# Ordering background reduction sums behind weight splits on VectorE, and their pace in one stage, in a one-layer transformer kernel

## The chip, the cores and the metric

The kernel runs on 1 core of one Trainium2 chip, as one program. The metric is device time in microseconds (us) from start to end of an execution, median over runs.

## The reference, cut to what matters

One decoder layer with 256 positions of width 2048, all in float32. A conditioning vector `c` gives six modulation vectors, which scale and shift the input and gate the output of two sub-layers:

```python
mod = jax.nn.silu(c) @ w_ada[l] + b_ada[l]
sh1, sc1, g1, sh2, sc2, g2 = jnp.split(mod[:, None, :], 6, axis=-1)
h = x * (1.0 + sc1) + sh1
y = token_mixer(h, w_in[l], conv_w[l], a_log[l], dt_bias[l], gdn_norm_w[l], rel_bias,
                w_proj_moba[l], w_proj_gdn[l], w_out[l])
x = layer_norm(DEEPNORM_ALPHA * x + g1 * y, ln1_g[l], ln1_b[l])
h = x * (1.0 + sc2) + sh2
y = swiglu(h, w_ffn_in[l], w_ffn_out[l])
x = layer_norm(DEEPNORM_ALPHA * x + g2 * y, ln2_g[l], ln2_b[l])
```

`token_mixer` projects `h` with `w_in` (13344 columns) into the inputs of a softmax attention, a gated delta rule (GDN) and two gates, runs the two mixers, projects both, merges them with the gates and projects with `w_out`. `swiglu` has a width of 5632. The product `silu(c) @ w_ada` is a matrix (2048 x 12288, 100 MB) times one vector.

## The kernel before, in words

**Weights in two parts.** TensorE multiplies in a reduced float32 form, so every weight tile of 128 x 1024 elements (512 KB) is split. `load_w` (L212) loads it into one of five `raw` slots through the Sync queue (L215). `split_w` (L218) makes `hi`, a cast on ScalarE (L222), and `lo`, the low part, raw minus hi, on VectorE (L223); `hi` and `lo` have four slots each. A raw slot comes free when both have been made. The matmuls use hi and lo with a high and a low part of the activations: three matmuls where one would do.

**Steps.** The program is a list `prog` of steps (L279), one weight tile each: the first function loads and splits the tile, the second issues its matmuls (24 with 256 columns or 12 with 512) and calls `tick`. `run(3)` (L285) goes through the list and loads and splits tiles up to three steps ahead of the step whose matmuls are issued.

**Background work.** `tick` (L177) moves background generators on, one lane after the other: `moba` and `main` and `pre` (attention, GDN), then `ada`. After each piece of `ada`, that lane rests for `pace["gap"]` steps: gap 2 means a piece every second step. The gap is 2 at first, 1 from `merge_begin` (L1042), and 4 from `ffn_more` (L1282).

**The modulation sums.** `silu(c) @ w_ada` isn't done on TensorE. For each of 96 blocks of 128 columns, VectorE multiplies the transposed block with `cb`, which holds `silu(c)` on every partition, and sums along the row (`ada_sum`, L238, instruction at L242). The first 40 blocks come early, by `ada_opening` with whole blocks in buffers of their own. The other 56 come in halves of 128 x 1024 by the lane `ada`: `ada_sums` (L246) loads a half into a `raw` slot (L253), the same five slots that the weight tiles use, and issues the sum of the half loaded one piece before. That makes 112 sums. Five generators of eight blocks (80 sums) belong to the first sub-layer and the second modulation, one of sixteen blocks (32 sums) is queued in `ffn_more`.

**Who fixes the order.** The kernel's text gives a program order. A scheduler in the compiler then lays down, engine by engine, an order of instructions for good: it takes, by a model of durations, what it holds to be ready, the earlier in program order first. The chip executes each engine's instructions in that order. `keep_in_program_order` pins an instruction; a manual dependency without semaphore ("NoSync") between two instructions of one engine makes the scheduler place the one behind the other, and adds nothing to be executed.

**The stages**, in order of time: the opening (modulation of the first blocks and the first weight tiles of `w_in`), up to about 270 us; attention and GDN as background of the rest of `w_in` and of `w_proj_moba`; `w_proj_gdn` with the merge (from about 750 us; `merge_begin` after the eighth of its 32 steps); the output projection with `w_out` (from about 876 us), in blocks of 512, 512, 512, 256 and 256 columns; the feed-forward part. `out_begin` (L1079) stands ahead of the output projection: it finishes the first generator of `ada`, sends the gate `g1` as a row to DRAM and back to all partitions (L1074 to L1077, queue of GpSimd), and sets up buffers. `mod2` (L1113), ahead of the fourth block, drains the lane `ada` and works out the second modulation (L1115 to L1118).

Other lines that the text names: L585 and L589 (the decay of the GDN), L653 (squared norms of the GDN's q and k; it frees a PSUM buffer), L762 (matmuls of the GDN's triangular inverse), L868 (normalization of the GDN's output, 16 instructions in a row), L354 to L356 (matmuls with 512 columns), L305 to L307 (with 256).

Of the kernel before, what the change touches and what calls it, by code (L numbers as in the profile page):

```python
# [13 lines left out]
OP = mybir.AluOpType  # L14
# [78 lines left out]
def layer(ctx, tc, a, out):  # L93
    nc = tc.nc
    v_, s_, g_, t_, dma = nc.vector, nc.scalar, nc.gpsimd, nc.tensor, nc.sync
# [21 lines left out]
    cols = perm.tile([P, V_END], F32, name="cols")  # L117
# [9 lines left out]
    cb = perm.tile([P, D], F32, name="cb")  # L127
# [30 lines left out]
    adac = perm.tile([P, 96], F32, name="adac")  # L158
# [4 lines left out]
    pace = {"all": 1.8, "gap": 2, "debt": 0.0}  # L163
    done = set()

    def advance(lane):
        while bg[lane]:
            try:
                return next(bg[lane][0])
            except StopIteration:  # L170
                bg[lane].pop(0)
        return None
# [39 lines left out]
    def load_w(w, k0, kn, c0, cn):  # L212
# [2 lines left out]
        dma.dma_start(raw[:, :kn * cn], w.tile(k0, kn, c0, cn))  # L215
        return v

    def split_w(raw, kn, cn, pin=False):  # L218
        hi = wp.tile([P, 1024], F32R, tag="hi", name="hi", bufs=4)
        lo = wp.tile([P, 1024], F32R, tag="lo", name="lo", bufs=4)  # L220
        hi, lo = [t[:, :kn * cn].rearrange("p (k n) -> p k n", n=cn) for t in (hi, lo)]
        s_.copy(hi, raw)  # L222
        low = v_.tensor_tensor(lo, raw, hi.bitcast(F32), op=OP.subtract)  # L223
        if pin:
            tc.keep_in_program_order(low)
        return hi, lo

    def split(hi, lo, src, scale=None):
# [9 lines left out]
    def ada_sum(col, part, raw, parts):  # L238
        first, last = part == 0, part == parts - 1
        n = D // parts  # L240
        h = ada_half[:, col % 4:col % 4 + 1]
        v_.tensor_tensor_reduce(out=raw, in0=raw, in1=cb[:, n * part:n * part + n], scale=1.0,  # L242
                                scalar=cols[:, col:col + 1] if first else h, op0=OP.mult, op1=OP.add,
                                accum_out=adac[:, col:col + 1] if last else h)

    def ada_sums(order, ahead):  # L246
        todo = [(col, half) for col in order for half in range(2)]
        held = []
        for n in range(len(todo) + ahead):
            if n < len(todo):  # L250
                col, half = todo[n]
                raw = wp.tile([P, 1024], F32, tag="raw", name="raw_a", bufs=5)
                dma.dma_start(raw, w_ada.tile(8 * half, 8, col * P, P, by_column=True))  # L253
                held.append((col, half, raw))
            if n >= ahead:
                ada_sum(*held.pop(0), 2)
                yield 1.35

    def ada_opening(order, ahead, at_once, between):
        held, loaded = [], 0  # L260
        for n, col in enumerate(order):
            while loaded < min(at_once if n < at_once else n + ahead + 1, len(order)):
                raw = ring[loaded % len(ring)]
                dma.dma_start(raw, w_ada.tile(0, KT, order[loaded] * P, P, by_column=True))
                held.append(raw)
                loaded += 1
                between(loaded)
            raw = held.pop(0)
            parts = 1 if n else 2
            for i in range(parts):  # L270
                ada_sum(col, i, raw[:, D // parts * i:D // parts * (i + 1)], parts)
            yield
# [6 lines left out]
    def step(w, k0, kn, c0, cn, post, begun=0, pin=False):  # L279
        prog.append((lambda: split_w(load_w(w, k0, kn, c0, cn), kn, cn, pin), post, begun))  # L280

    def do(fn):
        prog.append((None, fn, 0))
# [123 lines left out]
    def g8(slot, nm, shape, dt=F32):  # L407
        return k1.tile(shape, dt, tag=f"g{slot}", name=nm)
# [533 lines left out]
    def begin():  # L942
        ya = perm.tile([P, 2, MH, S], F32R, tag="s2", name="ya")
        for x in range(2):
            ya_ops[x].extend(ya[:, x, k, :] for k in range(MH))
        bg["pre"] += [gdn_pre(0), gdn_pre(1), gdn_norm(0)]
        bg["main"] += [gdn_chain(0), gdn_chain(1), gdn_turn(0), gdn_norm(1), gdn_turn(1)]
        bg["moba"] += [moba(0), moba(1)]
        bg["ada"] += [ada_sums(ada_order[n:n + 8], 1) for n in range(2 * KT + EARLY, len(ada_order), 8)]
# [120 lines left out]
    def bcast_row(v, dst):  # L1070
        ps = pt.tile([P, 512], F32, tag="tp", name="tpr")
        t_.transpose(ps[:KT, :P], adac[:, 16 * v:16 * v + 16], ident)
        rw = cur["k3"].tile([KT, P], F32, tag="up", name="rw", bufs=2) if "k3" in cur else e2("rw", [KT, P])
        v_.tensor_copy(rw, ps[:KT, :P])  # L1074
        rd = dr.tile([KT, P], F32, name=f"rd{v}")
        sdma.dma_start(rd, rw)
        sdma.dma_start(dst, rd.rearrange("r p -> (r p)").partition_broadcast(P))  # L1077

    def out_begin():  # L1079
        while len(bg["ada"]) > 4:  # L1080
            advance("ada")
        cur["g1b"] = g8(1, "g1b", [P, D])
        bcast_row(2, cur["g1b"])
        cur["r"] = perm.tile([P, 2, D], F32, tag="s2", name="r")
        cur["st"] = perm.tile([P, 2, 5, 6], F32, tag="stt", name="st1", bufs=2)

    do(out_begin)

    def resid(ps, c0, cn, gb, base, dst, st, n):
# [158 lines left out]
    begun, held = len(prog), []  # L1248
# [28 lines left out]
    def ffn_more():  # L1277
        act(0, pairs_of(pss[0]), pairs_of(pss[1]))
        act(1, pairs_of(pss[2]), pairs_of(pss[3]))
        bg["main"].append(ln1_affine())  # L1280
        bg["ada"].append(ada_sums(range(5 * KT, 6 * KT), 1))
        pace["gap"] = 4  # L1282
# [149 lines left out]
```

## Time and profile before

| what | value |
|---|---|
| three runs | 1716.8, 1734.97, 1738.95 us; median 1734.97 |
| the profiled execution's own time | 1726.41 us |
| its span on the core | 1724.6 us |
| TensorE matmul busy | 1675.8 us (97%) |
| VectorE busy | 1204.2 us (70%) |
| ScalarE busy | 796.9 us (46%) |
| moved by DMA | 417.58 MB, mean 242 GB/s |

How to read it: PE is TensorE, PEld its weight loads, DVE VectorE, ACT ScalarE, POOL GpSimd, SP the Sync engine, whose queue issues the loads. A row `L223 DVE ... lo<-raw,hi` is the instruction of line 223, which writes `lo` from `raw` and `hi`; `x134` is a count. In the timeline a row has start, duration, engine, line; in square brackets stands how long the engine was idle before it and what ended that. In the list of waits a row has who waited, for whom, the total in us, how often, and the longest. The chain of waits is followed back from the last instruction to what released it. In a table of windows the rows give the window, its length, each engine's busy time with its count, the clock granted to TensorE (1.00 is full), the busy share of the 16 DMA engines, and GB/s.

### The profile page before, as it was taken

To read this page: it belongs to the slowest core of one execution; us is meant where nothing else is said; L and a number is where in the kernel's file an instruction comes from. 1 tells how busy PE (TensorE), PEld (TensorE's weight loads), DVE (VectorE), ACT (ScalarE), POOL (GpSimd) and SP (SyncE) were. 2 spreads that over 40 slices of the span, in tenths; PEclk is the share of its full clock that TensorE was granted. 3 is DMA by queue.
4 is the path that set the end of the run, shared out by engine and by line. 5 is a ranking of instruction groups with operands and counts; after the bars stand their busy time and mean duration, and the time that the engine had idled before them with its cause. 6 is when DMAs were issued, how large, how long until landed. Compare 5 with 4: busy or idle time off the path is not lost.

```text
span 1724.6 us, 30521 instructions
## 1 busy us (share of the span) xinstructions
PE 1675.8 (97%) x12409; PEld 1571.8 (91%) x12409; DVE 1204.2 (70%) x1695; ACT 796.9 (46%) x1054; POOL 39.5 (2%) x61
## 2 busy tenths in 40 slices
PE   6999999999999999999989999999999999999999
PEld 4889999989899778999968999999999999888897
DVE  6899997999655786568976785655555544455454
ACT  3544445878445445464334454444444444333332
POOL 0000010010100001000000000000000000000000
PEclk9999999999999999999999999999999999999999
DMA  9999986565866678668997477777777766766652
GB/s 366 342 363 354 337 324 231 184 214 166 257 219 219 216 234 290 220 222 287 333 323 236 149 245 251 234 232 226 235 237 237 221 187 191 235 196 183 202 189 98
DMA packets 114305, 417.58 MB, mean 242 GB/s; under 512 B 13406, under 2 KB 14414, under 8 KB 108656
## 3 DMA queue, kind: packets, MB, share of 16 engines
q1 hardware_dynamic: 109652, 400.12, 69.3%
q0 software_dynamic: 4512, 15.51, 3.2%
q8 instruction: 97, 1.59, 0.4%
q14 instruction: 44, 0.36, 0.1%
HBM read 408.14 MB, written 7.44 MB: 241 GB/s over the span
## 4 chain that ended last, share of the span: by engine, by line
PE 79%; DVE 9%; DMA 7%; issue 3%; ACT 2%; SPq 0%; POOL 0%; DVEq 0%; ACTq 0%; POOLq 0%
PE mm L314 9%; PE mm L313 9%; PE mm L317 9%; PE mm L307 8%; PE mm L305 8%; PE mm L306 8%; PE mm L355 6%; PE mm L356 6%; PE mm L354 6%; DVE lo L223 4%; DMA raw_a<-in_w_ada 3%; DVE r L242 1%; DMA raw<-in_w_proj_gdn 1%; PE ps L762 1%; ACT hi L222 1%
## 5 line engine op out<-in xcount | busy, mean ns | idle before, releaser
L222 ACT CAST hi<-raw 128x1024 fp32r<-128x1024 f32 (+2 forms) x572 | 581.8, 1020 | 790.9 <-PE mm L314 243.5
L223 DVE TENSOR_TENSOR lo<-raw,hi 128x1024 fp32r<-128x1024 f32 (+2 forms) x572 | 672.0, 1183 | 292.7 <-ACT hi L222 292.2
L305 PE MATMUL mm<-s,hi 128*128 128x256 f32 x1184 | 337.6, 285 | 6.3 <-ACT hi L222 6.2
L307 PE MATMUL mm<-s,lo 128*128 128x256 f32 x1184 | 332.5, 282 | 8.4 <-DVE lo L223 8.4
L306 PE MATMUL mm<-s,hi 128*128 128x256 f32 x1184 | 331.6, 280 | 0.0
L314 PE MATMUL mm<-h,hi 128*128 128x256 f32 x1280 | 308.8, 281 | 0.0
L313 PE MATMUL mm<-h,hi 128*128 128x256 f32 x1280 | 308.7, 281 | 0.0
L313 PEld LDWEIGHTS mm<-h,hi 128*128 128x128 f32 x1280 | 242.3, 189 | 0.0
L314 PEld LDWEIGHTS mm<-h,hi 128*128 128x128 f32 x1280 | 241.6, 189 | 0.0
L307 PEld LDWEIGHTS mm<-s,lo 128*128 128x128 f32 x1184 | 225.5, 191 | 11.9 <-DVE lo L223 10.7
L305 PEld LDWEIGHTS mm<-s,hi 128*128 128x128 f32 x1184 | 225.9, 191 | 11.3 <-ACT hi L222 8.6
L306 PEld LDWEIGHTS mm<-s,hi 128*128 128x128 f32 x1184 | 226.1, 191 | 0.3
L317 PE MATMUL mm<-h,lo 128*128 128x256 f32 x1280 | 176.8, 281 | 0.0
L317 PEld LDWEIGHTS mm<-h,lo 128*128 128x128 f32 x1280 | 162.5, 189 | 0.0
L354 PE MATMUL mm<-hi,ach 128*128 128x512 f32 (+1 forms) x352 | 127.7, 363 | 0.0
L356 PE MATMUL mm<-hi,acl 128*128 128x512 f32 (+1 forms) x352 | 127.6, 363 | 0.0
L355 PE MATMUL mm<-lo,ach 128*128 128x512 f32 (+1 forms) x352 | 127.6, 363 | 0.0
L242 DVE CUSTOM_DVE_ANT_0 raw_a<-raw_a,cb,cols 128x1024 f32<-128x1024 f32 x56 | 71.8, 1282 | 69.3 <-DMA raw_a<-in_w_ada 69.3
L242 DVE CUSTOM_DVE_ANT_0 raw_a<-raw_a,cb,ada_half 128x1024 f32<-128x1024 f32 x56 | 71.8, 1282 | 65.2 <-DMA raw_a<-in_w_ada 65.2
L242 DVE CUSTOM_DVE_ANT_0 r<-r,cb,cols 128x2048 f32<-128x2048 f32 (+1 forms) x40 | 92.4, 2318 | 8.6 <-DMA r<-in_w_ada 8.6
L355 PE MATMUL mm<-lo,s 128*128 128x512 f32 x192 | 76.9, 401 | 2.8 <-DVE lo L223 2.7
L354 PE MATMUL mm<-hi,s 128*128 128x512 f32 x192 | 76.9, 402 | 0.0
(338 smaller groups left out, 2517.7 us busy)
## 6 DMA issues: line engine op xcount, KB each, us to landing
raw<-in_w_ffn_in SPq DMA_DIRECT2D x176, 512.0 KB, 4.0
raw<-in_w_in SPq DMA_DIRECT2D x168, 512.0 KB, 4.6
raw_a<-in_w_ada SPq DMA_DIRECT2D x112, 512.0 KB, 4.6
raw<-in_w_ffn_out SPq DMA_DIRECT2D x88, 512.0 KB, 4.3
r<-in_w_ada SPq DMA_DIRECT2D x40, 1024.0 KB, 8.3
raw<-in_w_proj_gdn SPq DMA_DIRECT2D x32, 512.0 KB, 4.6
raw<-in_w_out SPq DMA_DIRECT2D x32, 512.0 KB, 5.0
raw<-in_w_in SPq DMA_DIRECT2D x40, 384.0 KB, 5.7
```

Of the source, the lines that this page charges most:

```text
L222: s_.copy(hi, raw)
L223: low = v_.tensor_tensor(lo, raw, hi.bitcast(F32), op=OP.subtract)
L242: v_.tensor_tensor_reduce(out=raw, in0=raw, in1=cb[:, n * part:n * part + n], scale=1.0, scalar=cols[:, col:col + 1] if first else h, op0= ...
L305: t_.matmul(o, hi[:, i, c], ah, start=(first and i == 0 and t == 0), stop=False)
L306: t_.matmul(o, hi[:, i, c], al, start=False, stop=False)
L307: t_.matmul(o, lo[:, i, c], ah, start=False, stop=(last and i == kn - 1 and t == 1))
L313: t_.matmul(o, w, ops[0][k0 + i], start=(first and i == 0 and t == 0), stop=False)
L314: t_.matmul(o, w, ops[1][k0 + i], start=False, stop=False)
L317: t_.matmul(ps[:, t * S:(t + 1) * S], lo[:, i, t * P:(t + 1) * P], ops[0][k0 + i], start=False, stop=(last and i == kn - 1 and t == 1))
L354: t_.matmul(box[h], xh, hi[:, i, :], start=start, stop=False)
L355: t_.matmul(box[h], xh, lo[:, i, :], start=False, stop=False)
L356: t_.matmul(box[h], xl, hi[:, i, :], start=False, stop=stop)
```

## The change

Two things. First, `split_w` keeps each low part's instruction in a list, and `ada_sums` remembers, with each half that it loads, the last low part issued so far in program order, which is that of the tile three steps ahead of the current step. When the half's sum is issued, a NoSync dependency orders it on VectorE behind that low part. Second, `out_begin` sets the gap to 2, so that in the output projection a sum goes out every second step instead of every step.

```diff
+    lows = []
+
+    def behind(ins, first):
+        tc.add_manual_dep(ins.ins, first.ins.name,
+                          mybir.DependencyInfo(mybir.DependencyClass.NoSync, mybir.DependencyReason.DATA),
+                          reason="behind")
+
     def split_w(raw, kn, cn, pin=False):
...
         if pin:
             tc.keep_in_program_order(low)
+        lows.append(low)
         return hi, lo
...
-        v_.tensor_tensor_reduce(out=raw, in0=raw, in1=cb[:, n * part:n * part + n], scale=1.0,
+        return v_.tensor_tensor_reduce(out=raw, in0=raw, in1=cb[:, n * part:n * part + n], scale=1.0,
...
                 dma.dma_start(raw, w_ada.tile(8 * half, 8, col * P, P, by_column=True))
-                held.append((col, half, raw))
+                held.append((lows[-1], (col, half, raw)))
             if n >= ahead:
-                ada_sum(*held.pop(0), 2)
+                low, args = held.pop(0)
+                behind(ada_sum(*args, 2), low)
                 yield 1.35
...
         cur["st"] = perm.tile([P, 2, 5, 6], F32, tag="stt", name="st1", bufs=2)
+        pace["gap"] = 2
 
     do(out_begin)
```

More of the change, by code (lines that the diff above doesn't have):

```diff
@@ L241, in ada_sum @@
         h = ada_half[:, col % 4:col % 4 + 1]
-        v_.tensor_tensor_reduce(out=raw, in0=raw, in1=cb[:, n * part:n * part + n], scale=1.0,
-                                scalar=cols[:, col:col + 1] if first else h, op0=OP.mult, op1=OP.add,
-                                accum_out=adac[:, col:col + 1] if last else h)
+        return v_.tensor_tensor_reduce(out=raw, in0=raw, in1=cb[:, n * part:n * part + n], scale=1.0,
+                                       scalar=cols[:, col:col + 1] if first else h, op0=OP.mult, op1=OP.add,
+                                       accum_out=adac[:, col:col + 1] if last else h)
     def ada_sums(order, ahead):
```

## The prediction

> **What bounds the kernel now.** I read the page first, then windows, then who waited for whom, then the chain of waits inside the one stretch where TensorE stood still longest.
>
> ```profile
> span 1724.6 us, 30521 instructions
> PE 1675.8 (97%) x12409; PEld 1571.8 (91%) x12409; DVE 1204.2 (70%) x1695; ACT 796.9 (46%) x1054; POOL 39.5 (2%) x61
> PE 79%; DVE 9%; DMA 7%; issue 3%; ACT 2%; SPq 0%; POOL 0%; DVEq 0%; ACTq 0%; POOLq 0%
> L242 DVE CUSTOM_DVE_ANT_0 raw_a<-raw_a,cb,cols 128x1024 f32<-128x1024 f32 x56 | 71.8, 1282 | 69.3 <-DMA raw_a<-in_w_ada 69.3
> L242 DVE CUSTOM_DVE_ANT_0 raw_a<-raw_a,cb,ada_half 128x1024 f32<-128x1024 f32 x56 | 71.8, 1282 | 65.2 <-DMA raw_a<-in_w_ada 65.2
> ```
>
> TensorE is the bound: 97% busy, 48.8 us idle. The reader is to see that VectorE stands idle 69.3 + 65.2 = 134.5 us in front of the 112 sums, always for the sum's own tile. That is far more than TensorE's whole idle time, so most of it costs nothing; the question is where it does. TensorE's waits, first between 276 and 900 us, then between 440 and 700 us, name the places:
>
> ```profile
> PE ps_c L589 <- DVE w L585: 1.6, 1, 1.6
> PE mm L354 <- ACT hi L222: 2.6, 1, 2.6
> ...
> PE ps L762 <- DVE kqn L653: 3.8, 1, 3.8
> PE mm L355 <- DVE lo L223: 2.7, 2, 1.8
> PE mm L307 <- DVE lo L223: 2.3, 1, 2.3
> ```
>
> From 900 us on there is little: the feed-forward stages keep TensorE busy through, as in the last row of the next fence, although VectorE waits for sums there too. The windows around the stalls (columns: length, then busy time and instructions of PE, PEld, DVE, ACT, POOL, granted clock, DMA share, GB/s):
>
> ```profile
> 467.00:474.00 7.00, 6.19 (x29) 6.19 (x30) 3.42 (x8) 0.58 (x1) 0.00 (x0) 0.51 0.74 221
> 628.00:631.00 3.00, 1.18 (x5) 0.67 (x4) 3.00 (x6) 0.69 (x1) 0.00 (x0) 0.98 0.51 139
> 631.00:634.00 3.00, 3.00 (x8) 2.32 (x8) 2.83 (x7) 0.35 (x1) 0.00 (x0) 0.50 0.90 285
> 658.00:662.00 4.00, 4.00 (x21) 4.00 (x21) 3.16 (x3) 1.04 (x1) 0.25 (x1) 0.57 0.95 315
> 790.00:876.00 86.00, 83.49 (x666) 78.97 (x665) 76.61 (x102) 33.87 (x36) 1.01 (x2) 1.00 0.91 318
> 876.00:895.00 19.00, 15.65 (x56) 12.11 (x55) 10.83 (x15) 4.44 (x5) 0.09 (x1) 0.82 0.95 334
> 887.00:894.00 7.00, 6.24 (x16) 4.95 (x16) 4.35 (x6) 2.09 (x2) 0.00 (x0) 0.52 0.90 289
> ...
> 1150.00:1175.00 25.00, 25.00 (x215) 25.00 (x214) 14.63 (x15) 10.55 (x11) 0.00 (x0) 1.00 0.77 236
> ```
>
> So each stall is paid twice: behind it the granted clock is about 0.5 for a few microseconds. And from 790 to 895 us the stage is another one: 318 to 334 GB/s, DMA engines over 0.9 busy.
>
> Why VectorE is late at 463 us is in its timeline and in the chain of waits from 440 to 470 us:
>
> ```profile
> 448.83 2.35 DVE L223 TENSOR_TENSOR lo<-raw,hi 128x1024 fp32r<-128x1024 f32 x2
> 457.18 1.28 DVE L242 CUSTOM_DVE_ANT_0 raw_a<-raw_a,cb,ada_half 128x1024 f32<-128x1024 f32 x1 [6.00 <-DMA raw_a<-in_w_ada]
> ...
> 458.99 2.35 DVE L223 TENSOR_TENSOR lo<-raw,hi 128x1024 fp32r<-128x1024 f32 x2
> 465.73 1.28 DVE L242 CUSTOM_DVE_ANT_0 raw_a<-raw_a,cb,cols 128x1024 f32<-128x1024 f32 x1 [4.39 <-DMA raw_a<-in_w_ada]
> ...
> 467.54 0.22 DVE L653 TENSOR_SCALAR kqn<-ss,epsc 128x8 f32<-128x8 f32 x1
> 467.67 1.21 DVE L223 TENSOR_TENSOR lo<-raw,hi 128x1024 fp32r<-128x1024 f32 x1
> ```
>
> ```profile
> 448.91 1.14 DVE lo L223
> 450.07 6.97 DMA raw_a<-in_w_ada
> ...
> 459.07 1.15 DVE lo L223
> 460.23 5.36 DMA raw_a<-in_w_ada
> ```
>
> This is a ring. A load waits for one of the five shared `raw` slots; the slot comes free when a low part has run; the low part stands on VectorE behind a sum; the sum waits for its own load, issued only now. One turn takes 10.2 us (450.07 to 460.23) and covers two steps.
>
> ```profile
> 500.00:525.00 25.00, 25.00 (x223) 25.00 (x222) 14.27 (x16) 10.70 (x14) 0.00 (x0) 1.00 0.77 255
> L223 DVE TENSOR_TENSOR lo<-raw,hi 128x1024 fp32r<-128x1024 f32 x134 | 162.3, 1218 | 23.3 <-ACT hi L222 22.9
> L222 ACT CAST hi<-raw 128x1024 fp32r<-128x1024 f32 x134 | 140.3, 1049 | 218.5 <-PE mm L306 115.4 <-DMA raw<-in_w_proj_gdn 24.9 <-PE mm L356 22.3
> ```
>
> TensorE needs 24 x 25 / 223 = 2.69 us for a step of 24 matmuls, 5.4 us for two. A ring turn of 10.2 us eats the three prepared steps, and at 463 us they are gone: TensorE waits for a small L653 that is queued behind the sum of 465.73.
>
> **The change part by part.** No instruction or DMA is added or removed: 112 sums of 1.28 us and their loads stay.
>
> Part 1, the edges. Each sum now stands behind the low part of the last weight tile loaded before its own. In the old order, counting loads and low parts, most sums stand three low parts ahead of that point (the sum of 457.18: its load of 450.07 follows the load of weight tile 159, counted from 0, whose low part runs at 467.67). That tile's load was issued earlier, so when its low part can run the sum's tile has mostly landed too. Behind a waiting sum are then only low parts of tiles loaded after it. Most of the 134.5 us should go; what it is worth on TensorE:
> - 463 us: the stall of 3.8 us, and the clock of 0.51 for 7 us, 7 x 0.49 = 3.4 us of work. Two sums with 6.00 and 4.39 us of waiting are its whole cause. Bounds 0 and 7.2; I take 7.2.
> - 628 to 662 us: stalls of 2.7 and 2.3 us, clock 3.0 x 0.50 + 4.0 x 0.43 = 3.2 us; together 8.2. The ring is there too, but so are other works in front of the low parts (next fence). Bounds 0 and 8.2; I take half, 4.1.
> - 294 us: the wait of 1.6 us for L585, in whose queue sums also stand; bounds 0 and 1.6, I take 0.8.
> - Feed-forward stage, 32 sums: its waits are hidden behind prepared steps today; 0.
>
> ```profile
> 652.52 4.29 DVE L868 SCALAR_TENSOR_TENSOR yb<-bv,ors,yb 128x128 f32<-128x128 f32 x16
> 615.00:628.00 13.00, 13.00 (x57) 10.36 (x56) 11.12 (x21) 6.23 (x7) 0.00 (x0) 1.00 0.82 257
> ```
>
> The price of part 1 is slots: a sum that stands later gives its slot back later.
>
> ```profile
> DMA to landing us min/median/max: 3.1/4.6/8.6
> ```
>
> That is `raw_a`'s own row. With a sum every second step, two steps take 3 loads through 5 slots, so a slot may be held 5/3 x 5.4 = 9.0 us. A weight tile needs 4.6 to land, 1.05 cast, 1.22 low part: 6.9 us. A sum's tile needs about the same, since it lands after its weight tile and adds its 1.28 behind it. So the cover is 2 us a slot plus the prepared steps; it is gone when landings take over 9.0 - 2.3 = 6.7 us for long. With a sum every fourth step (feed-forward) a slot may be held 5/5 x 10.8 us: safe.
>
> In the merge stage the gap is 1: 2 loads a step, 5/2 x 2.69 = 6.7 us a slot, less than 6.9. Loads fall behind there today, and sums already stand behind their low parts. The edges change little in that order, but the stage is entered with fewer loads ahead. Bounds 0 and 3 us lost (two landed tiles less, at 524288 B / 334 GB/s = 1.57 us each); I take 1.5.
>
> Part 2, the gap of 2 from the first step of the output projection. By counting, six sums and five of their loads are left then; they go out over 12 steps instead of 6, of the 24 before `mod2`, which therefore finds nothing to drain.
>
> ```profile
> 873.92 0.33 SPq L215 DMA_DIRECT2D raw<-in_w_out  x1
> 875.66 0.33 SPq L253 DMA_DIRECT2D raw_a<-in_w_ada  x1
> 876.86 0.33 SPq L215 DMA_DIRECT2D raw<-in_w_out  x1
> 878.00 0.33 SPq L253 DMA_DIRECT2D raw_a<-in_w_ada  x1
> 875.52 0.57 POOL L1077 DMA_DIRECT2D g1b<-rd  x1 [4.16 <-DMA rd<-rw]
> 876.86 8.45 DMA raw<-in_w_out
> ```
>
> The weight tile issued at 876.86 takes 8.45 us, beside the broadcast of the gate row and the sums' tiles, and TensorE waits 2.6 us for its cast (the second row of the waits) and runs at 0.52 for 7 us (3.4 us). One sum load less ahead of it gives 1.57 us, and of the clock stretch perhaps half, 1.7: 3.3 us. Bounds 0 (the broadcast alone is enough to stop it) and 6.0; I take 3.3.
>
> Sum: 7.2 + 4.1 + 0.8 - 1.5 + 3.3 = 13.9 us. Against the profiled execution's own 1726.4 us (span 1724.6) that is 1712.5, rounded to 1712. The median of the runs shown, 1735.0, is 8.6 above that execution; a run like it may carry more of the same stalls, which this change would remove, so I don't add it.
>
> The Trainium skill, "TensorE: Matmul & The Clock Gate", section "Why this matters for your kernels", advises against PE-idle gaps over about 3 us, since an idle window brings the clock to half. The trace agrees on the half clock but not on that length: stalls of 1.8 and 2.3 us are followed by clocks of 0.50 and 0.57. By the rule alone, those two clock stretches would have another cause and stay, and the sum would be 1.6 us smaller (half of 3.2), about 1714.
>
> **The rivals.**
> - *The waits were cover, not cause.* TensorE waits for other VectorE work: for it speak L868's 4.29 us of unbroken work and 11.12 of 13 us busy at 615; against it the ring at 450. Then a stall of like size opens elsewhere, and only some of part 2 is left: about 1725.
> - *Everything goes.* All bounds in full, 7.2 + 8.2 + 1.6 + 6.0 = 23.0 us, and nothing lost at the slots: about 1703. For it: the ring runs through 440 to 660 us; against: the merge stage stays at its DMA limit.
> - *Slots run out (slower).* Sums hold their slots longer from 430 to 790 us, and landings above 6.7 us turn the slots into the bound. At 8.45 us a slot is held 8.45 + 2.3 = 10.75 us, two steps take 3/5 x 10.75 = 6.45 instead of 5.4, a loss of 1.07 us a pair. If one pair in six of the some 65 there is so slow and the 463 us stall also stays, 11 x 1.07 = 12 us and two new half-clock stretches of 1.7: 1726.4 + 15.4 - 3.3 = 1738.5. For it: landings of 6.97 and 8.45 us; against: the median of 4.6, and that VectorE no longer adds its own wait to a slot.
> - *The order doesn't bind*, because the scheduler had the sums there already: only true of the merge stage; then about 1723. I count it with the first rival.
>
> **How the numbers follow.** Forecast 0.54, waits as cover 0.17, everything goes 0.16, slots run out 0.13. The range 1697 to 1739 leaves out the fast end of the third case and the slow end of the last. Its low end is "everything goes" with a few us of luck in stalls that the profile doesn't show. Faster by over 2% means below 1700.3 against the median, which only "everything goes" can reach: 0.12. Slower by over 2% means over 1769.7: 0.05, a slot shortage much worse than priced. Within 2%, about what a measurement of this kernel can tell from no change: 0.83.
>
> **What would show it.** Right: VectorE's idle time before L242 falls from 134.5 us to under 40; no 3.8 us wait for L653 and no half clock near 467; fewer `raw_a` pieces in the chain between 440 and 660; sums of the output projection alternating with two weight loads. Wrong: TensorE waits for low parts or casts that wait for `raw` between 440 and 790 us; a longer stop at 850 to 895 us; the half-clock stretches still there in the same number.

## The result and the profile after

| | before | after |
|---|---|---|
| median of 22 executions | 1715.38 us (1705.75 to 1738.95) | 1698.89 us (1692.7 to 1719.5) |
| profiled execution, its own time | 1726.41 us | 1699.4 us |
| its span | 1724.6 us | 1697.6 us |

The ratio of the runs, after to before, is 0.9922, 95% interval 0.9896 to 0.9949. That is 1715.4 x 0.0078 = 13.4 us faster (8.7 to 17.8). The ratio leaves out executions that are over 1.5% above the fastest of their kernel, six of before and one of after, and so says less than the medians, which lie 16.5 us apart. The two profiled executions are 27.0 us apart, twice as much; where the rest comes from is worked out below.

The page of the changed kernel first (its span, the busy times, the costliest VectorE group), then the row of the sums in the groups by line (both halves). Line numbers are higher by 7 at the casts, 8 at the sums, 9 further down: the low part is L230, the cast L229, the sum L250.

```profile
span 1697.6 us, 30506 instructions
PE 1651.1 (97%) x12409; PEld 1548.3 (91%) x12409; DVE 1205.1 (71%) x1695; ACT 795.7 (47%) x1052; POOL 40.1 (2%) x61
L230 DVE TENSOR_TENSOR lo<-raw,hi 128x1024 fp32r<-128x1024 f32 (+2 forms) x572 | 673.7, 1184 | 385.4 <-ACT hi L229 384.4
```

```profile
L250 DVE CUSTOM_DVE_ANT_0 raw_a<-raw_a,cb,cols 128x1024 f32<-128x1024 f32 x56 | 71.6, 1278 | 2.3 <-DMA raw_a<-in_w_ada 2.3
L250 DVE CUSTOM_DVE_ANT_0 raw_a<-raw_a,cb,ada_half 128x1024 f32<-128x1024 f32 x56 | 71.6, 1278 | 0.2
```

The idle time in front of the sums was 69.3 + 65.2 = 134.5 us and is 2.3 + 0.2 = 2.5 us. It did not turn into work: VectorE is as busy as before, and now idles more in front of the low parts (385.4 us, waiting for the cast, against 292.7 before). What changed is who stands behind whom when VectorE waits. TensorE's waits between 276 and 900 us (who waited, for whom, total, times, longest):

```profile
PE mm L316 <- DVE lo L230: 4.7, 5, 2.1
PE ps L771 <- DMA TT<-ubd: 3.5, 1, 3.5
PE mm L364 <- DVE lo L230: 2.1, 3, 0.8
PE mm L363 <- ACT hi L229: 1.9, 1, 1.9
```

The wait of 3.8 us for the GDN's small L653 is gone; a new one of 3.5 us, for a transfer into `TT`, stands in the list. The windows, with the columns as before:

```profile
467.00:474.00 7.00, 7.00 (x69) 6.80 (x68) 2.71 (x4) 4.09 (x9) 0.50 (x1) 1.00 0.59 209
649.00:654.00 5.00, 1.55 (x12) 1.34 (x11) 2.52 (x3) 0.11 (x1) 0.00 (x0) 0.95 1.00 365
653.00:657.00 4.00, 3.59 (x17) 3.59 (x18) 1.52 (x3) 1.53 (x2) 0.00 (x0) 0.57 1.04 422
820.00:872.00 52.00, 48.67 (x350) 44.05 (x350) 46.01 (x61) 19.24 (x20) 1.10 (x2) 1.00 0.95 332
875.00:882.00 7.00, 6.24 (x15) 4.66 (x16) 6.28 (x8) 3.14 (x3) 0.00 (x0) 0.53 0.86 324
1150.00:1175.00 25.00, 25.00 (x223) 25.00 (x222) 16.28 (x18) 10.79 (x12) 0.00 (x0) 1.00 0.75 241
```

At 467 us TensorE is busy through at full clock. At 649 us and near 875 us it still stops, with the half clock behind.

Where VectorE stood in the ring, its timeline now reads (start, duration, and in brackets the idle time before it):

```profile
451.01 1.23 DVE L230 TENSOR_TENSOR lo<-raw,hi 128x1024 fp32r<-128x1024 f32 x1 [0.28 <-ACT hi L229]
452.15 1.28 DVE L250 CUSTOM_DVE_ANT_0 raw_a<-raw_a,cb,cols 128x1024 f32<-128x1024 f32 x1
...
457.15 0.23 DVE L662 TENSOR_SCALAR kqn<-ss,epsc 128x8 f32<-128x8 f32 x1 [0.98 <-PE ss L660]
457.30 1.22 DVE L230 TENSOR_TENSOR lo<-raw,hi 128x1024 fp32r<-128x1024 f32 x1
...
458.50 1.28 DVE L250 CUSTOM_DVE_ANT_0 raw_a<-raw_a,cb,ada_half 128x1024 f32<-128x1024 f32 x1
```

Each sum stands behind a low part and runs without waiting. The small L662 (L653 before) now runs at once: TensorE's last L660, which it reads, ends at 457.12 us, and it starts at 457.15. In the kernel before the same result was there at 457.25 us, and L653 ran at 467.54, behind the sum of 465.73. So it is in all traces of this case: it runs 9.3 to 11.0 us after its input in the four without edges and with shared slots, and 0.03 to 0.04 us after it in the nine with edges.

**Where the time came from.** In both traces the start of the same TensorE weight load can be taken and subtracted. The table gives what was gained in each stretch, for the two profiled executions above and for a second pair (each kernel profiled once more, in the experiments below):

| from matmul that starts at (before) | first pair | second pair |
|---|---|---|
| 269.8 to 307.9 us | 0.8 | 2.8 |
| 307.9 to 462.4 us | -1.2 | 0.2 |
| 462.4 to 508.3 us | 7.0 | 4.3 |
| 601.9 to 661.6 us | 5.1 | 2.2 |
| 661.6 to 701.3 us | -5.4 | -2.3 |
| 827.6 to 857.9 us (merge) | -0.3 | 0.2 |
| 857.9 to 917.1 us (output projection) | 1.9 | 5.6 |
| start to 956.7 us, all | 9.4 | 12.2 |
| 993.0 to 1480.0 us (feed-forward) | 17.6 | -17.6 |
| 1480 us to the end | 0.0 | 0.0 |

The change is the part up to 957 us: 9.4 and 12.2 us. The second pair gains more near 875 us, where the changed kernel's second trace has no half clock at all (6.83 us of it in the first). The feed-forward part has nothing to do with the change, since it goes the other way in the second pair. There the first matmuls (L313, L314 and L317, with 256 columns; L322 to L326 after) start every 117.8 ns in the profiled execution of before and every 113.3 ns in that of after, 1.07 us per 240 of them at a granted clock of 1.00. The window row at 1150 us shows it as x215 before and x223 after. The second pair has it reversed: 113.3 before, 117.8 after.

**What is late next at 649 us.** The chain of waits of the changed kernel between 600 and 660 us, and GpSimd's queue in the same stretch, after and then before:

```profile
638.25 6.49 DMA ubd<-mt
...
645.15 8.21 DMA TT<-ubd
...
653.41 3.68 PE ps L771 x16
```

```profile
630.65 1.43 POOL L754 DMA_DIRECT2D ubd<-Ub  x1 [50.26 <-DVE Ub L750]
638.25 1.09 POOL L755 DMA_DIRECT2D ubd<-mt  x1 [6.18 <-DVE ors L410]
...
645.15 0.89 POOL L762 DMA_DIRECT2D TT<-ubd  x1 [4.91 <-DMA ubd<-mt]
```

```profile
644.66 1.43 POOL L745 DMA_DIRECT2D ubd<-Ub  x1 [57.09 <-DVE Ub L741]
650.19 1.09 POOL L746 DMA_DIRECT2D ubd<-mt  x1 [4.11 <-DVE or L397]
...
656.48 0.89 POOL L753 DMA_DIRECT2D TT<-ubd  x1 [4.30 <-DMA ubd<-mt]
```

The GDN writes a triangular matrix to DRAM and reads it back transposed, on GpSimd's queue. From the first write to the issue of the read into `TT` took 656.48 - 644.66 = 11.8 us before and 645.15 - 630.65 = 14.5 us after. Before, that was hidden: TensorE, late by the stalls of 628 to 662 us, came to L762 at 662.23 us without a wait. With those stalls gone it comes to L771 at 649.96 and stands until 653.41. So the 5.1 us won up to there are handed back: 3.5 us of wait and 1.7 us of half clock (4.0 x 0.43).

### The profile page after: what moved, and what is told of

The parts are those of the page before. It is cut to its first block, busy times and chain, and to the rows that moved or that the text cites. A ratio compares the mean times of both kernels' runs of the same rounds, so it can differ in the third digit from the quotient of the medians.

```text
span 1697.6 us, 30506 instructions
## 1 busy us (share of the span) xinstructions
PE 1651.1 (97%) x12409; PEld 1548.3 (91%) x12409; DVE 1205.1 (71%) x1695; ACT 795.7 (47%) x1052; POOL 40.1 (2%) x61
## 4 chain that ended last, share of the span: by engine, by line
PE 80%; DVE 7%; issue 5%; DMA 5%; ACT 2%; POOL 0%; SPq 0%; ACTq 0%; DVEq 0%; POOLq 0%
PE mm L316 9%; PE mm L314 9%; PE mm L323 9%; PE mm L326 9%; PE mm L322 9%; PE mm L315 8%; PE mm L364 6%; PE mm L365 6%; PE mm L363 6%; DVE lo L230 3%; DMA raw<-in_w_proj_gdn 2%; PE ps L771 1%; DVE r L250 1%; ACT hi L229 1%; DMA r<-in_w_ada 1%
## 5 line engine op out<-in xcount | busy, mean ns | idle before, releaser
L230 DVE TENSOR_TENSOR lo<-raw,hi 128x1024 fp32r<-128x1024 f32 (+2 forms) x572 | 673.7, 1184 | 385.4 <-ACT hi L229 384.4
L229 ACT CAST hi<-raw 128x1024 fp32r<-128x1024 f32 (+2 forms) x572 | 582.7, 1022 | 769.2 <-PE mm L323 228.3
L314 PE MATMUL mm<-s,hi 128*128 128x256 f32 x1184 | 335.3, 283 | 7.5 <-ACT hi L229 7.3
L316 PE MATMUL mm<-s,lo 128*128 128x256 f32 x1184 | 330.1, 280 | 7.9 <-DVE lo L230 7.8
L322 PE MATMUL mm<-h,hi 128*128 128x256 f32 x1280 | 298.0, 276 | 0.0
L323 PE MATMUL mm<-h,hi 128*128 128x256 f32 x1280 | 298.0, 276 | 0.0
L322 PEld LDWEIGHTS mm<-h,hi 128*128 128x128 f32 x1280 | 240.2, 188 | 0.0
L314 PEld LDWEIGHTS mm<-s,hi 128*128 128x128 f32 x1184 | 223.6, 189 | 12.9 <-ACT hi L229 10.1
L316 PEld LDWEIGHTS mm<-s,lo 128*128 128x128 f32 x1184 | 223.1, 189 | 11.4 <-DVE lo L230 10.1
L315 PEld LDWEIGHTS mm<-s,hi 128*128 128x128 f32 x1184 | 223.7, 189 | 0.3
L326 PE MATMUL mm<-h,lo 128*128 128x256 f32 x1280 | 171.1, 276 | 0.0
L326 PEld LDWEIGHTS mm<-h,lo 128*128 128x128 f32 x1280 | 156.9, 188 | 0.0
L250 DVE CUSTOM_DVE_ANT_0 r<-r,cb,cols 128x2048 f32<-128x2048 f32 (+1 forms) x40 | 92.5, 2320 | 10.8 <-DMA r<-in_w_ada 10.7
L365 PEld LDWEIGHTS mm<-hi,acl 128*128 128x128 f32 x352 | 66.4, 189 | 10.4
L363 PEld LDWEIGHTS mm<-hi,ach 128*128 128x128 f32 x352 | 66.4, 189 | 10.4
```

The costliest lines, as they stand in the source:

```text
L250: return v_.tensor_tensor_reduce(out=raw, in0=raw, in1=cb[:, n * part:n * part + n], scale=1.0, scalar=cols[:, col:col + 1] if first else ...
L314: t_.matmul(o, hi[:, i, c], ah, start=(first and i == 0 and t == 0), stop=False)
L315: t_.matmul(o, hi[:, i, c], al, start=False, stop=False)
L316: t_.matmul(o, lo[:, i, c], ah, start=False, stop=(last and i == kn - 1 and t == 1))
L322: t_.matmul(o, w, ops[0][k0 + i], start=(first and i == 0 and t == 0), stop=False)
L323: t_.matmul(o, w, ops[1][k0 + i], start=False, stop=False)
```

## The experiments

The theory: the order on VectorE costs the time; behind a waiting sum stood work that TensorE needed, and the edges alone bring most of the gain. The rivals: the gain is the gap in the output projection; the sharing of slots is the cause, not the order; the wait at 649 us is one execution's accident. Stage figures below are taken from pairs of traces as in the table above.

**One part alone: the edges.** The changed kernel without its last line:

```diff
-        pace["gap"] = 2
```

> The edges alone, gap in the output projection as before. Theory (the edges break the ring of load, sum, low part and slot near 463 us; the gap is worth about 2 us): 10 to 14 us faster than before, the 3.8 us wait of TensorE near 463 us gone, and the stop near 875 us as long as before, 2.5 us and 6.8 us at half clock. Rival (the gap carries the gain): within 3 us of before.

Measured: 1701.49 us (12 runs), ratio to before 0.9952 (0.9913 to 0.9991). Its rows (VectorE's wait, then TensorE's waits from 276 to 900 us, then a window):

```profile
DVE raw_a L250 <- DMA raw_a<-in_w_ada: 3.6, 1, 3.6
```

```profile
PE mm L364 <- DVE lo L230: 3.4, 6, 0.8
PE mm L363 <- ACT hi L229: 2.6, 1, 2.6
```

```profile
648.00:657.00 9.00, 8.15 (x71) 7.86 (x69) 5.89 (x8) 5.71 (x8) 0.00 (x0) 1.00 1.02 411
```

The edges alone are worth 0.0048 x 1715 = 8.2 us (1.5 to 14.9) of the 13.4; they remove VectorE's waits and the stall at 463 us, and leave the wait for the cast near 872 us at the 2.6 us that it had before. There is no wait for `TT` here, and in this trace the edges alone gain 13.7 us up to 957 us, more than the change in its first trace.

**The other part alone: the gap.** The kernel before with that line added:

```diff
+        pace["gap"] = 2
```

> The gap of 2 in the output projection alone, no edges. Theory: 1 to 3 us faster than before, with the 3.8 us wait near 463 us still there. Rival (the gap carries the gain): 10 us faster or more.

Measured: 1709.76 us (12 runs), ratio 0.9983 (0.9953 to 1.0012). VectorE waits as before, and the stretch at 463 us is lost as in the old kernel:

```profile
DVE raw_a L242 <- DMA raw_a<-in_w_ada: 152.9, 69, 6.1
```

```profile
463.00:474.00 11.00, 7.57 (x44) 7.07 (x43) 4.37 (x7) 2.87 (x4) 0.00 (x0) 0.71 0.75 252
```

TensorE's stop there is put down to `TT` (2.6 us) first and to L653 (0.8 us) after it; L653 runs at 470.74 us, 11.0 us after its input. Between these two kernels the stretch 464.8 to 510.2 us is 6.5 us apart. So the gain at 463 us belongs to the edges. The gap alone is not told from nothing.

**Edges without the feed-forward part.** The changed kernel, its last 32 sums without an edge:

```diff
-                behind(ada_sum(*args, 2), low)
+                total = ada_sum(*args, 2)
+                if "k3" not in cur:
+                    behind(total, low)
```

> The change without the edges of the last 32 sums, those of the feed-forward part. In the two profiles the matmuls there came every 117.8 ns before and every 113.4 ns after, 17 us in all. Theory (the edges there are worth nothing; the pace differs from execution to execution, whatever the kernel): the same time as the change, within 3 us, and either pace in its profile. Rival (the edges of the feed-forward part bring the faster pace): about 17 us slower than the change, with 117.8 ns.

Measured: 1698.17 us (10 runs), ratio 0.9925 (0.988 to 0.997), the changed kernel's own.

```profile
DVE raw_a L250 <- DMA raw_a<-in_w_ada: 64.4, 32, 4.1
```

All 32 sums wait again, 64.4 us in all, and TensorE loses nothing: from 1040 to 1677 us the two traces differ by 0.00 us. This is VectorE idle time that costs nothing, beside the same kind of idle time at 463 us that cost 7.

**More room for the round trip.** The changed kernel, the GDN lane resting two steps longer before the second block's first L771:

```diff
-            yield rest(((10,5),(14,7))[b][hh])
+            yield rest(((10,5),(16,7))[b][hh])
```

> The change, with the second GDN half waiting 16 instead of 14 steps between its round trip through DRAM and the matmuls that need it. Theory (what the edges win between 602 and 649 us is given back because TensorE now comes to these matmuls before the round trip has landed, 3.5 us and 3.4 us at half clock): that wait is gone, and it is 3 to 5 us faster than the change. Rival (the wait stands for other late work there): the wait goes to another place and the time stays within 1 us of the change.

Measured: 1710.27 us (12 runs), ratio 0.9941 (0.9903 to 0.9978). The wait for `TT` is gone, and the stretch from 649 to 728 us is 8.4 us shorter than in the changed kernel's trace; 2.7 us come back by 763 us, and the trace was 5.7 us behind when it came to 649 us. Executions of this kernel fall into two groups, 1691.6 to 1699 and 1710 to 1712.5 us, as the changed kernel's do (1692.7 to 1700 and 1710.3 to 1719.5); 7 of 12 are in the upper one here and 9 of 22 there, which moves the median. By time it can't be told from the change.

**A slot of their own for the sums.** The kernel before, weight tiles in four `raw` slots, the sums in one of their own (two were not tried):

```diff
-        raw = wp.tile([P, 1024], F32, tag="raw", name="raw", bufs=5)
+        raw = wp.tile([P, 1024], F32, tag="raw", name="raw", bufs=4)
...
-                raw = wp.tile([P, 1024], F32, tag="raw", name="raw_a", bufs=5)
+                raw = wp.tile([P, 1024], F32, tag="rawa", name="raw_a", bufs=1)
...
-        bg["ada"].append(ada_sums(range(5 * KT, 6 * KT), 1))
+        bg["ada"].append(ada_sums(range(5 * KT, 6 * KT), 0))
```

(the other generators likewise with 0, and the row buffer that shares the slots with four).

> The kernel before, without edges and with gap 1 in the output projection, but the sums' halves load into one slot of their own, the weight tiles share four, and a sum is issued with its own load instead of one piece later. It opens the ring at the slot and leaves the sums ahead of the low parts. Theory (the ring needs the shared slot: the sum waits for a load that waits for a low part behind the sum): VectorE's waits for the halves fall well under half of the 134.5 us, and the 3.8 us wait of TensorE near 463 us is gone; four slots for the weights may cost some microseconds in the opening. Rival (the place on VectorE alone counts, whatever the slots): waits of 100 us or more, and the wait near 463 us is there.

Measured: 1736.03 us (4 runs), ratio 1.0143 (1.0091 to 1.0196), slower. The expectation fell: with one slot a sum's load waits for the sum before it, and the two make a ring of their own, as its chain of waits from 440 to 470 us shows:

```profile
449.32 4.30 DMA raw_a<-in_w_ada
453.65 1.28 DVE raw_a L242
454.97 4.99 DMA raw_a<-in_w_ada
459.99 1.28 DVE raw_a L242
```

VectorE still waits 119.1 us for the halves, which is the rival's sign; no wait for L653 is left, which is the theory's. TensorE's waits from 276 to 900 us went elsewhere:

```profile
PE ps L762 <- DMA TT<-ubd: 12.9, 2, 8.1
PE ps_c L589 <- DVE w L585: 5.8, 1, 5.8
```

It says that one slot is too few for the sums. Whether the shared slots are needed for the ring, it does not settle; that sharing alone isn't the cause is shown by the edges, which keep it and end the waits.

**A nearer edge.** The changed kernel with each sum behind the low part two tiles earlier:

```diff
-                held.append((lows[-1], (col, half, raw)))
+                held.append((lows[-3], (col, half, raw)))
```

> The change with each sum behind the low part of the tile two before the last one loaded ahead of its half, so only one place later than before instead of three. Theory (what counts is that the low part a sum stands behind cannot run before the half has landed): VectorE's waits for the halves come back in part, 30 to 100 us, and the time lies between the change and before, some 3 to 10 us slower than the change. Rival (any edge does, since it only stops the scheduler from putting sums at the earliest place): waits under 10 us and the time of the change.

Measured: 1706.59 us (10 runs), ratio 0.9978 (0.9942 to 1.0015), by the ratios 0.0056 x 1713 = 9.6 us worse than the change (the two intervals overlap by 0.0007).

```profile
DVE raw_a L250 <- DMA raw_a<-in_w_ada: 32.8, 23, 3.1
```

```profile
PE ps L771 <- DMA TT<-ubd: 8.2, 1, 8.2
```

```profile
648.00:657.00 9.00, 1.87 (x10) 1.38 (x8) 8.13 (x13) 3.31 (x4) 1.77 (x2) 0.82 0.84 292
```

VectorE's waits lie between the two kernels (134.5, 32.8, 2.5 us), and the stall at 463 us is gone already. The loss in this trace is the wait for `TT`, 8.2 us, with the half clock behind it. How the waits of the sums make the round trip later was not traced to one instruction, so the dose is shown for VectorE's waits, and not as a straight line in the time.

**Both kernels profiled again.** The kernel before, unchanged, and the changed kernel, unchanged, one execution each.

> The kernel before once more, for its profile alone. Theory (the long wait for L653 near 463 us belongs to the order of this kernel): a wait of some microseconds on the GDN's matmuls and 6.8 us at half clock between 460 and 475 us again, either pace in the feed-forward part, and 1706 to 1717 us with the faster, 1722 to 1739 us with the slower. Rival (it was an accident of one execution): no such wait.

Measured: 1708.33 us. Its TensorE waits from 276 to 900 us and two windows:

```profile
PE ps L762 <- DVE kqn L653: 3.1, 1, 3.1
PE ps L762 <- DMA TT<-ubd: 2.6, 1, 2.6
```

```profile
463.00:474.00 11.00, 7.92 (x55) 7.73 (x55) 4.37 (x7) 2.68 (x4) 0.00 (x0) 0.84 0.72 267
1150.00:1175.00 25.00, 25.00 (x223) 25.00 (x222) 14.47 (x15) 11.10 (x12) 0.00 (x0) 1.00 0.75 245
```

The wait for L653 recurs, at 3.1 us, with 3.41 us of half clock instead of the 6.8 expected: the wait belongs to the old order. A wait for `TT` is seen here too, 2.6 us.

> The change once more, for its profile alone. Theory (the wait of 3.5 us for the round trip near 649 us is an accident of landing times, as four kernels with the same edges had none and three had one): no wait near 463 us, and at 649 us either. Rival (the wait at 649 us belongs to the order of the change): again 3 us or more.

Measured: 1713.68 us.

```profile
PE ps L771 <- DMA TT<-ubd: 3.6, 2, 3.2
```

```profile
1150.00:1175.00 25.00, 25.00 (x215) 25.00 (x214) 14.24 (x15) 10.52 (x12) 0.00 (x0) 1.00 0.72 230
```

The wait for `TT` recurs in both traces of the changed kernel, so it is no accident of one execution. But it hangs on landing times too. Six traces have the same order on every engine up to 750 us: these two, and those with the edges alone, without feed-forward edges, and with gap 2 in the whole merge or from its middle (both below). In three of them the read into `TT` that TensorE needs first landed after 8.2, 7.7 and 8.8 us, and TensorE waited 3.2 to 3.7 us (the changed kernel twice, gap 2 in the whole merge); in the other three it landed after 5.7, 5.5 and 5.4 us, and TensorE did not wait for it.

**The merge stage at gap 2.** The changed kernel without the line in `merge_begin`:

```diff
-        pace["gap"] = 1
```

> The change without the gap of 1 in the merge stage: gap 2 throughout, so that some six sums are left over and are drained at once ahead of the fourth block of the output projection. Theory (the merge stage is held by its loads: two tiles a step through five slots): TensorE no longer waits for casts and low parts between 820 and 880 us, no half clock near 875 us, 5 to 9 us faster than the change less what the drain costs, 0 to 4 us. Rival (the merge stage is held by VectorE's work on the merge): the waits there stay and the time is that of the change or longer.

Measured: 1705.42 us (12 runs), ratio 0.9926 (0.9886 to 0.9966). Against the changed kernel's trace the merge gains 3.4 us and the start of the output projection 8.8, and 4.6 are given back from 907 to 947 us, where `mod2` now has sums to drain; against the changed kernel's second trace, without half clock near 875 us, the first two are 3.0 and 4.9 us. By the ratios it is not told from the change (0.9926 and 0.9922).

**Gap 2 from the middle of the merge.** The changed kernel, the gap set to 2 already ahead of the sixth of the merge's eight blocks, twelve steps before its end:

```diff
     for j in range(4, 8):
+        if j == 5:
+            do(lambda: pace.update(gap=2))
         ws_unit(ybT, w_pg, 256 * j, KT, merge(j))
```

> The change with the gap set to 2 already after 12 of the 24 steps of the merge stage, so that 12 sums are left for the 24 steps ahead of the second modulation and nothing has to be drained. Theory (loads hold the merge stage): 4 to 8 us faster than the change, half clock near 875 us gone. Rival (VectorE holds it): within 1 us of the change.

Measured: 1695.58 us (12 runs), ratio 0.9915 (0.988 to 0.995); the profiled execution took 1687.39 us.

```profile
820.00:872.00 52.00, 51.08 (x362) 47.28 (x362) 43.60 (x54) 21.84 (x23) 1.11 (x2) 1.00 0.95 350
875.00:882.00 7.00, 7.00 (x32) 5.82 (x31) 6.88 (x11) 3.42 (x4) 0.00 (x0) 1.00 0.89 313
```

Against the rows of the changed kernel: busy through where that one stopped, no half clock near 875 us, 1.6 + 8.8 = 10.4 us less between 820 and 907 us, and nothing to drain later. Against the changed kernel's second trace, which has no half clock near 875 us either, it is 6.1 us. By the ratios of the runs it is not told from the change (0.9915 and 0.9922). Its executions fall into two groups too, 1685.9 to 1690.8 and 1700.4 to 1708.2 us, each below the like group of the change (1692.7 to 1700.0 and 1710.3 to 1719.5); but the two kernels ran in different sessions, and in this one's the median of before was 2.4 us lower.

**The same early gap without edges.** The kernel before, with both gaps of the kernel above and none of the edges:

```diff
+        if j == 5:
+            do(lambda: pace.update(gap=2))
...
+        pace["gap"] = 2
```

> No edges, gap 2 from 12 steps into the merge stage on. Theory (edges and pace are independent: the edges are worth some 12 us, the early gap some 8 with the 2 of the late one): 7 to 10 us faster than before, half clock near 885 us gone, the wait near 463 us still there. Rival (the early gap only pays with the edges): within 3 us of before.

Measured: 1713.38 us (10 runs), ratio 1.0004 (0.9969 to 1.0039). The 7 to 10 us that were expected did not come, though in its trace the wait of 3.8 us for L653 near 463 us is down to 0.3, behind one of 2.2 us for `TT`. Its TensorE waits from 276 to 900 us:

```profile
PE mm L355 <- DVE lo L223: 7.2, 5, 2.6
PE mm L307 <- DVE lo L223: 4.6, 4, 2.1
```

The two longest of L355, 2.6 us at 649 us and 2.1 us at 886 us, are for low parts behind sums that waited 3.0 and 4.3 us for their halves; the longest of L307, at 657 us, is for one behind the 16 normalizations. A half clock of 3.41 us stays at 886 us, where none was expected. The same two gaps with edges give 0.9915, whose interval ends at 0.995, below this one's start: with these gaps too, the edges are what pays. That the early gap pays on top of the edges is seen in traces and not told by the runs (0.9915 against 0.9952 for the edges alone, with intervals that overlap).

**The normalization behind low parts too.** The kernel with the early gap, and the 16 instructions of L877 ordered behind the last low part, four at a time with a larger cost for the lane:

```diff
-                v_.scalar_tensor_tensor(ys, o[:, i, h, :], rs[:, i, h:h + 1], ys, op0=OP.mult, op1=OP.mult)
+                behind(v_.scalar_tensor_tensor(ys, o[:, i, h, :], rs[:, i, h:h + 1], ys, op0=OP.mult, op1=OP.mult),
+                       lows[-1])
...
-                yield 1.1
+                yield 1.9
```

> The kernel with the edges and gap 2 after 12 steps of the merge stage, and besides the 16 normalizations of a GDN half (4.29 us in one block on VectorE) spread over more steps, four a step, each behind the low part of the tile last loaded. Theory (the wait of 2.1 us for a low part near 641 us is that block, and the 3.4 us at half clock follow from it): both gone, 3 to 4 us faster than that kernel without the spread. Rival (TensorE there waits for the late round trip or ScalarE anyway): the wait moves and the time stays within 1 us.

Measured: 1697.88 us (6 runs), ratio 0.9897 (0.9832 to 0.9962); the profiled execution took 1685.53 us.

The block in the changed kernel's VectorE timeline, and then TensorE's wait for low parts from 276 to 900 us in this kernel (2.1 us at the longest in that one):

```profile
638.80 4.29 DVE L877 SCALAR_TENSOR_TENSOR yb<-bv,ors,yb 128x128 f32<-128x128 f32 x16
```

```profile
PE mm L316 <- DVE lo L230: 2.2, 4, 0.8
```

The stop of 2.1 us behind the block is gone, and no half clock is left between 40 and 1681 us. The trace is 1.9 us shorter than that of the kernel with the early gap; the runs don't tell the two apart.

## Why the prediction held, step by step

The time was predicted at 1712 us and 13.9 us below the profiled execution. Measured: 13.4 us faster by the ratio, and 1698.9 us. The difference was right, though its terms were not all, and that 13.9 and 13.4 lie so close is luck in part: the two pairs of traces give 9.4 and 12.2 us, and the medians 16.5. The level was not right, since the base was high: the profiled execution of 1726.4 us had the slower feed-forward pace, which costs 17.6 us, and the median of 22 executions of before is 1715.4. The three runs shown, with a median of 1735.0, pointed the other way.

- **463 us, 7.2 taken.** 7.0 in the first pair, 4.3 in the second. The old kernel's stall varies with it (3.8 and 3.1 us, and a half clock of 6.83 and 3.41 us). Shown by the two parts run alone: 6.5 us apart here.
- **628 to 662 us, 4.1 taken.** This is the step that failed. 5.1 and 2.2 us were won and 5.4 and 2.3 given back within 40 us: nothing net. "I take half" named no work that would be late next. It was the round trip through DRAM on GpSimd's queue, whose start lies 11.8 to 14.5 us ahead of the issue of the read into `TT`, and the block of L877 (4.29 us from 638.80), whose stop of 2.1 us stayed, as the first rival had it. Where that read lands early, in the three traces of the same order without the wait, the stretch from 601.9 to 701.3 us gains 4.3 to 4.5 us against the first trace of before. So the term is worth nothing or some 4.4 us, by the landing of one read, and a half of the bound that comes near the second is luck.
- **294 us, 0.8 taken.** 0.8 and 2.8, between 269.8 and 307.9 us.
- **Feed-forward, 0 taken.** Right: without its edges there the kernel has the change's ratio and stages.
- **Price of slots in the merge, 1.5 taken.** -0.3 and +0.2: within what two traces differ, so nothing. The sums do hold their slots longer, 11.7 us on average from a load's issue to the end of its sum against 6.6 before (loads from 430 to 790 us of the first pair; the prediction took about 6.9), but the weight tiles hold theirs shorter, 12.0 against 14.6 us, and nothing runs short; the rival "slots run out" did not happen.
- **The gap in the output projection, 3.3 taken.** 1.9 and 5.6 in the pairs; the gap alone gives 0.9983, which is 2.9 us with an interval that includes zero. In this stretch its trace is 3.3 and 3.1 us ahead of the two of before. The size was fair, the reason was not. The prediction had one sum load less ahead of the late weight tile, and that came: from 863.01 us on the Sync queue issues two weight tiles to a sum. The tile still lands late, as the chain of waits of the changed kernel from 870 to 880 us and GpSimd's queue show:

```profile
865.06 8.74 DMA raw<-in_w_out
```

```profile
865.40 0.57 POOL L1086 DMA_DIRECT2D g1b<-rd  x1 [4.52 <-DMA rd<-rw]
```

The broadcast of the gate row takes 9.48 us from 865.40, and the loads issued beside it take 8.7 to 9.1 us here, 8.4 to 8.7 before and 8.2 to 9.1 with the edges alone, whatever the gap. That is the lower bound which the prediction named, "the broadcast alone is enough to stop it"; no run moved the broadcast, so the cause is read from times that coincide. The stop is 1.9 us with 6.83 us of half clock in the first trace, and 1.7 us with none in the second, which is most of what parts 1.9 from 5.6. In the trace with gap 2 twelve steps earlier the loads there are as slow (7.7 to 9.1 us), but eight tiles of `w_out` were issued ahead of the broadcast, against six here, and TensorE does not stop.
- **Sum.** 7.0 + 5.1 - 5.4 + 0.8 - 0.3 + 1.9 and some small stretches give 9.4 in the first pair, 12.2 in the second; the runs give 13.4 (8.7 to 17.8).

Of the signs named, these came: idle time before the sums under 40 us (2.5), no wait for L653 and no half clock near 467 us, no `raw_a` load in the chain from 440 to 660 us (7 before), sums alternating with two weight loads in the output projection. The rival "waits were cover" is true of one place, 628 to 662 us, and not of the kernel.

Open: why the reads of `TT` take 5.7 us in one execution and 8.2 in another; what sets the pace of the feed-forward matmuls; and whether the broadcast makes the loads beside it late. No run here tried the last two.

## What to carry to other kernels

On an engine that executes in a fixed order, put background work that waits for its own transfer behind the foreground work whose transfer was issued earlier; the idle time in front of it then holds up less that is already due. Idle time of such an engine is worth only what stands behind it: of the 134.5 us here, 132 went for some 13 us of time, and the 64.4 us that stayed in the feed-forward part of the kernel without edges there cost nothing. Before a win is counted in full, ask what hidden round trip TensorE will reach earlier; and compare traces stretch by stretch, since two executions of one kernel can differ by more than the change.

## What the runs showed of the hardware

**Two paces of the same matmuls.** The 256-column matmuls of the first feed-forward product start every 113.3 ns or every 117.8 ns, one of the two for a whole execution, with the granted clock at 1.00 in both. Over 3840 of them that is 17.1 us of the 17.6 in the table. Each of the kernels before and after showed both, and of the fourteen profiled executions four had the slower one. The 22 executions of the changed kernel fall into two groups, 13 from 1692.7 to 1700.0 us and 9 from 1710.3 to 1719.5, and its two profiled ones (1699.4 at 113.3 ns, 1713.7 at 117.8) lie in the group that their pace says; that the pace makes the groups is an inference. The executions of before can be parted so as well, 12 from 1705.8 to 1716.8 and 10 from 1722.4 to 1739.0; the means of the lower groups then lie 15.8 us apart, those of the upper 16.9. No stage outside the first feed-forward product shows it.

**A stop costs a whole stretch of half clock or none.** The stretches of half clock inside the kernels last 3.41, 6.83 or 10.24 us, multiples of 3.41. The same stop of 2.1 us before L316, in front of the same matmul, is followed at once by one in three traces, among them the kernel without feed-forward edges (648 to 657 us at 0.82, the row below; its line is L318), and by none in four, among them the kernel with the edges alone (1.00):

```profile
648.00:657.00 9.00, 9.00 (x68) 9.00 (x67) 6.58 (x9) 4.60 (x6) 0.68 (x1) 0.82 0.98 363
```

The Trainium skill, "TensorE: Matmul & The Clock Gate", section "What's actually happening", has the clock follow how busy TensorE was lately, in windows of 3413 ns that run freely and do not start anew with the kernel. The lengths in these traces agree (3.41 us). It also fits that one and the same stop is caught in one execution and not in another, which makes 1.7 us (half of 3.41) of each stall's price a matter of where it falls.
